# Sample attention's cached values: from held values and 16 moving columns to held weights and moving values

## The chip, the cores and the metric

The kernel runs on one core of a Trainium2 chip. The metric is the device time of one execution in microseconds (us), from the start of the program to its end. Times "before" are the median of three executions without a profiler, 2341.11 us (2338.23 to 2343.40 us). Beside them stands one execution taken by the hardware profiler; its span runs from the first to the last instruction. The engines are PE (TensorE: matmuls; PEld is its load of the held operand), DVE (VectorE), ACT (ScalarE), POOL (GpSimd) and SP (SyncE, which issues the DMAs of this kernel).

## The reference

One layer of an encoder works on two kinds of rows: a prompt of 2048 frames, and a sample of 8 running streams with 16 new frames each, 128 rows together. Each sample stream attends to 512 cached keys and values of its own and to its 16 new frames. There are two branches: differential attention (4 heads, two score maps each, values 128 wide) and stick-breaking attention (8 heads, values 64 wide). The branches are gated, merged, projected, added to the input and normed.

```python
w = p[:, :, 0] - lam * p[:, :, 1]
o = jnp.einsum('bhqk,bkhe->bqhe', w, v, preferred_element_type=jnp.float32)
...
a = jnp.where(mask, jnp.exp(log_a), 0.0)
o = jnp.einsum('bhqk,bkhd->bqhd', a, v, preferred_element_type=jnp.float32)
...
oa = diff_attention(qa, jnp.concatenate([cache_a_k[l], ka], axis=1),
                    jnp.concatenate([cache_a_v[l], va], axis=1), pos_s, kpos_s, lam)
ob = stick_breaking_attention(qb, jnp.concatenate([cache_b_k[l], kb], axis=1),
                              jnp.concatenate([cache_b_v[l], vb], axis=1), pos_s, kpos_s)
```

The change touches the product of weights and cached values (the two einsums) for the sample's streams. All other parts stay.

## The kernel before, in words

The kernel splits each fp32 operand into two fp16 parts, a high and a low one, and replaces one fp32 matmul by three fp16 ones (high x high, high x low, low x high). Work goes by 17 tiles of 128 rows: 16 of the prompt (`t < NT`) and one of the sample (`t == NT`). The attention of the prompt is done by eight units `u`: even units (`kind` 0) are one head of differential attention, odd ones (`kind` 1) two heads of stick-breaking attention. A first stage prepares the inputs, a second one projects and runs the prompt's attention, and the last one, from about 1780 us of the profile on, merges the branches and projects tile by tile. Its matmuls are L1315 (`branches`), the transposes L1165 (`transposed`) and L1344 (`output`); `wo`, `wb`, `wa` hold split weights or activations.

The sample's attention is threaded through that last stage. `sample` returns 13 lists of pieces for each unit. They are put on a `lane`, a unit starting 6 steps (`S_PERIOD`) after the one before it, and `aside` hands the 55 lane steps out over the first 13 tiles of the stage; `interleave` mixes them with the pieces of the tile. The framework's scheduler then fixes the order of instructions of each engine; each engine works through its queue in order. SP's queue holds all loads and stores of this stage, the transposing DMAs among them.

A unit's lane steps are these. Step 0, `fetch`: the unit's own sample rows are loaded (`dsam`) and the scale factors `dsf` computed (L736 to L738). Steps 0 to 3 load the cached keys, two streams at a time (`cache`, L747, tile `dc`, 512 KB), steps 5 to 8 the cached values in the same way; keys and values share three buffers `dc`. `keys` splits keys (`k16c`, L290 on ACT and L295 on DVE) and turns them with a transposing DMA (`dks`, L754). `scores_all` (step 6) computes scores. There (L772) the held operand is the query, padded to 32 columns in `qpad`, each for one of four groups of 32 columns of PE that belongs to 32 partitions of the result, and 512 columns of keys are moved. Softmax or stick-breaking follow; `turn` splits the weights and turns them with a transposing DMA (`dwt`, L580): keys on partitions, 128 sample rows on columns, 5 blocks of high parts and 5 of low parts (four cached blocks of 128 keys and the new rows). `values` (steps 6 to 9) splits the values (`v16c`).

`output_cached(i)` (steps 8 to 11) computes the product for two streams at a time. A cached block of values is held (128 keys by 128 columns for an even unit, by 64 for each head of an odd one) and the 16 columns of weights of one stream are moved; 12 matmuls (3 pairs of parts, 4 blocks) add up one stream of one head (L803). The result stands turned, value columns on partitions and sample rows on columns, in the only buffer of PSUM tag "t"; ACT scales its 32 columns into `ot` (L806). `finish` (step 12) computes the part of the new rows into `o` (`pv_block`, `natural`), turns `ot` back on PE (L815) and adds it on DVE (L816); `store` sends `o` to `o_d`, from where the sample's tile, the last but one of the stage, takes it.

Of the kernel before, what the change touches and what calls it, by code (L numbers as in the profile page):

```python
# [16 lines left out]
F32 = mybir.dt.float32  # L17
# [3 lines left out]
AF = mybir.ActivationFunctionType  # L21
ALU = mybir.AluOpType
# [3 lines left out]
P = 128  # L26
# [4 lines left out]
NS = 16  # L31
# [6 lines left out]
STICK = 14  # L38
# [25 lines left out]
C_MAS = C_MB + 128  # L64
C_MBS = C_MAS + 128
C_SEL = C_MBS + 128
C_N = C_SEL + 256


def shape_constants():  # L70
    half = 32
    inv = (10000.0 ** (-np.arange(half, dtype=np.float64) / half)).astype(np.float32)
    pos = np.concatenate([np.arange(SEQ), np.tile(PAST + np.arange(NS), NB)]).astype(np.float32)
    ang = (pos[:, None] * inv[None, :]).astype(np.float64)
    cos = np.cos(ang).astype(np.float32).reshape(17, P, half).transpose(1, 0, 2)
# [12 lines left out]
    return c  # L88
# [21 lines left out]
def layer_kernel(ctx: ExitStack, tc: tile.TileContext, a: dict):  # L110
# [6 lines left out]
    def act(**kw):  # L117
# [16 lines left out]
        "av": a["cache_a_v"][0].rearrange("b (j p) h e -> p (b j) (h e)", p=P),  # L134
        "bk": a["cache_b_k"][0].rearrange("b (j p) h d -> p (b j) (h d)", p=P),
        "bv": a["cache_b_v"][0].rearrange("b (j p) h d -> p (b j) (h d)", p=P),
    }
    outs = {
        "ak": (a["out_2"][0, 0].rearrange("s h c d -> s (h c d)"),
# [47 lines left out]
    def bank(tag, dt=F32):  # L187
        return ps.tile([P, 512 if dt == F32 else 1024], dt, tag=tag, name=f"ps_{tag}", bufs=BANKS[tag])
# [530 lines left out]
    def cache_column(name, h):  # L719
        return ("ak", "av", "bk", "bv").index(name) * 4 + h  # L720

    def sample(U, dec, qpad, cs):


        kind, h, t, sc, sq = U["kind"], U["h"], NT, U["sc"], U["sq"]
# [5 lines left out]
        def fetch():  # L731

            box["s"] = sam = dec.tile([P, 8, P], F16, tag="dsam", name="dsam", bufs=2)
            load(out=sam, in_=s_d[U["u"]])
            box["f"] = f = dec.tile([P, 3], F32, tag="dsf", name="dsf", bufs=2)
            V.tensor_scalar(out=f[:, 0:1], in0=ik, scalar1=sq[:, 1:2], scalar2=0.125, op0=ALU.mult, op1=ALU.mult)  # L736
            V.tensor_scalar(out=f[:, 1:2], in0=ik, scalar1=sq[:, 1:2], scalar2=-0.125, op0=ALU.mult, op1=ALU.mult)
            V.tensor_scalar(out=f[:, 2:3], in0=iv, scalar1=ls[:, 1:2] if kind == 0 else 2.0 ** -STICK, scalar2=None, op0=ALU.mult)  # L738

        def queries():  # L740
            for r in range(2):
# [2 lines left out]

        def cache(name, i):
            box[name, i] = kc = dec.tile([P, 8, P], F32, tag="dc", name="dc", bufs=3)
            load(out=kc, in_=caches[name][:, i * 8 : i * 8 + 8, h * P : (h + 1) * P])  # L747

        def keys(i):
            kc = box.pop((nk, i))  # L750
# [36 lines left out]
            box["v", i] = v16 = dec.tile([P, 8, 2, P], F16, tag="v16c", name="v16c", bufs=2)  # L787
            split(v16[:, :, 0, :], v16[:, :, 1, :], vc, sv, S)

        def output_cached(i):  # L790

            if i == 0:
                box["ot"] = dec.tile([P, P], F32, tag="ot", name="ot")
            vs = box.pop(("v", i))
            po = bank("t")
            for b in range(2):
                cols = slice((2 * i + b) * NS, (2 * i + b + 1) * NS)
                for c, job in enumerate(box["jobs"]):
                    r = slice(c * 64, c * 64 + 64) if kind == 1 else slice(0, P)
                    n = 0  # L800
                    for vf, wf in ((0, 0), (0, 1), (1, 0)):
                        for j in range(4):
                            T.matmul(po[r, cols], vs[:, b * 4 + j, vf, r], job["segs"][0]["wt"][:, wf * 5 + j, cols], start=(n == 0), stop=(n == 11))  # L803
                            n += 1
            c = slice(i * 32, i * 32 + 32)
            S.activation(out=box["ot"][:, c], in_=po[:, c], func=AF.Identity, scale=box["f"][:, 2:3])  # L806

        def finish():
            po = bank("s")
            vn = box["s"][:, 6:8, :].rearrange("p c (f d) -> p c f d", f=2)  # L810
            for job in box["jobs"]:
                pv_block(job, job["segs"][0], po, 4, vn, True, True)
            o = natural(U, t, po, dec)
            pt = bank("t")
            T.transpose(pt[:, 0:P], box["ot"], ident)  # L815
            V.tensor_tensor(out=o, in0=o, in1=pt[:, 0:P], op=ALU.add)  # L816
            store(U, t, o)

        def one(fn, *args):
# [460 lines left out]
    with ExitStack() as c2:  # L1280
# [81 lines left out]

        qpad = res.tile([P, 4, NB, 32], F16, name="qpad")
        G.memset(qpad, 0.0)

        lane = []
        for u in range(8):
            for i, pieces in enumerate(sample(units[u], dec, qpad, cs)):
# [58 lines left out]
```

## Time and profile before

| what | us |
|---|---|
| three executions without the profiler: median (lowest, highest) | 2341.11 (2338.23, 2343.40) |
| span of the profiled execution | 2337.1 |
| PE busy in it | 2121.6 (91%) |
| DVE busy | 1707.5 (73%) |
| ACT busy | 1663.1 (71%) |
| POOL busy | 661.3 (28%) |
| first and last start of L803 | 1874.4 and 2216.0 |

A profiled execution's time outside the span isn't recorded; the median lies 4.0 us above this span. A row of a group names its line, engine, operation, output and inputs, shapes (partitions x elements) and count. A matmul's own length in the profile includes its way through the array, so that neighbours overlap; what a matmul costs in a stream is the distance from one start to the next.

### The profile page before, as it was taken

Reading aid. Unit: us, or ns where it says so; the run is one execution under the profiler, and the core shown is the slowest. Engines: PE = TensorE matmul, PEld = TensorE weight load, DVE = VectorE, ACT = ScalarE, POOL = GpSimd, SP = SyncE. Lnnn points to the kernel's source line nnn. Section 1 sums busy time; section 2 is a strip of 40 time slices with the busy share of each in tenths; the row PEclk is TensorE's granted clock in tenths of the full one; section 3 lists DMA queues with packets and bytes.
Section 4 is the critical chain, followed back from the end, with each engine's and each line's share of the span. In section 5 each row is a group of like instructions: output and inputs, shape, how many; then the busy total and the mean of one; then the engine's idle time right before and its main releaser. Section 6 shows DMA issues by size and latency. Waiting matters only on the chain. (4 is left out here: it accounts for less than half of the span.)

```text
span 2337.1 us, 42708 instructions
## 1 busy us (share of the span) xinstructions
PE 2121.6 (91%) x15272; PEld 1144.0 (49%) x15272; DVE 1707.5 (73%) x3653; ACT 1663.1 (71%) x3292; POOL 661.3 (28%) x578
## 2 busy tenths in 40 slices
PE   5998898998989899899999979999995878989998
PEld 3654454545545445445545545554553444544443
DVE  4658765779875677978667797777788777777663
ACT  4968777787877778778677777866777656756541
POOL 1222022356300334731024474103345111121111
PEclk7999999999999999999999999999997988999999
DMA  9777659897895898867577777756677999999521
GB/s 333 275 214 180 152 118 272 179 193 168 212 210 126 216 204 192 179 178 192 134 191 176 185 168 186 195 146 150 146 171 166 285 254 233 257 245 236 155 98 53
DMA packets 834358, 445.35 MB, mean 191 GB/s; under 512 B 537210, under 2 KB 777130, under 8 KB 833632
## 3 DMA queue, kind: packets, MB, share of 16 engines
q1 hardware_dynamic: 833196, 442.24, 76.0%
q8 instruction: 119, 1.95, 0.4%
q14 instruction: 95, 0.78, 0.1%
q10 hardware_dynamic: 948, 0.39, 0.1%
HBM read 245.60 MB, written 69.24 MB: 135 GB/s over the span
## 5 line engine op out<-in xcount | busy, mean ns | idle before, releaser
L622 POOL TENSOR_TENSOR sc_p<-sc_p,sc_n 128x127 f32<-128x127 f32 (+7 forms) x192 | 313.8, 1638 | 826.5 <-DVE sc_n L616 812.2
L428 PE MATMUL ps_mm<-wb,hs 128*128 128x512 f16 x1632 | 414.5, 382 | 1.5 <-DMA hs<-hT_d 1.3
L428 PEld LDWEIGHTS <-hs 128*128 128x128 f16 x3120 | 274.4, 98 | 257.3 <-DMA hs<-hT_d 11.8
L428 PE MATMUL ps_mm<-wa,hs 128*128 128x512 f16 x1488 | 374.6, 382 | 9.8 <-DVE qbuf L463 6.4
L616 DVE TENSOR_TENSOR_SCAN sc_n<-ps_s,sc_n,zero_t 128x512 f32<-128x512 f32 x192 | 245.4, 1278 | 68.4 <-ACT ps_s L119 65.0
L639 PE MATMUL ps_s<-k,qst 128*128 128x512 f16 (+3 forms) x640 | 224.2, 351 | 37.9 <-DVE sc_n L616 29.9
L573 DVE TENSOR_TENSOR sc_n<-sc_p,sc_n 128x128 f16<-128x128 f32 (+7 forms) x192 | 212.7, 1112 | 58.1 <-ACT sc_n L572 57.6
L504 PEld LDWEIGHTS <-hs 128*128 128x128 f16 x1632 | 156.6, 98 | 188.3 <-ACT qst L532 6.2
L119 ACT ACTIVATE sc_p<-ps_s,usc 128x512 f32<-128x512 f32 (+3 forms) x320 | 204.8, 640 | 30.2 <-PE ps_s L640 25.3
L640 PE MATMUL ps_s<-k,qst 128*128 128x512 f16 (+3 forms) x640 | 224.2, 352 | 0.0
L572 ACT CAST sc_n<-sc_p 128x128 f16<-128x128 f32 (+7 forms) x192 | 155.5, 813 | 78.5 <-POOL sc_p L622 76.9
L700 PE MATMUL ps_o<-v,wt 128*128 128x128 f16 x1088 | 171.5, 225 | 32.6 <-DMA wt<-sc_n 32.2
L119 ACT ACTIVATE ps_s<-ps_s,usc 128x512 f32<-128x512 f32 (+3 forms) x328 | 200.0, 610 | 0.0
L504 PE MATMUL ps_t<-wa,hs 128*128 128x512 f16 x816 | 192.9, 383 | 7.6 <-ACT qst L532 6.0
L504 PE MATMUL ps_t<-wb,hs 128*128 128x512 f16 x816 | 191.9, 380 | 1.2 <-DVE qst L532 0.8
L1344 PE MATMUL ps_o<-wo,wb 128*128 128x512 f16 x816 | 186.5, 383 | 4.1 <-ACT wb L1166 4.1
L701 PE MATMUL ps_o<-v,wt 128*128 128x64 f16 x1088 | 157.9, 197 | 0.0
L700 PEld LDWEIGHTS <-wt 128*128 128x128 f16 x1088 | 105.1, 101 | 98.1 <-DMA wt<-sc_n 45.1
L558 DVE TENSOR_SCALAR_CACHE_REDUCE sc_p<-ps_s,usc 128x512 f32<-128x512 f32 (+3 forms) x160 | 106.3, 665 | 42.4 <-PE ps_s L640 31.7
L616 DVE TENSOR_TENSOR_SCAN sc_n<-ps_s,zero_t 128x128 f32<-128x128 f32 (+3 forms) x128 | 104.1, 814 | 44.0 <-ACT ps_s L119 43.4
L558 DVE TENSOR_SCALAR_CACHE_REDUCE sc_n<-ps_s,usc 128x512 f32<-128x512 f32 (+3 forms) x160 | 106.3, 665 | 36.9 <-PE ps_s L640 26.3
L701 PEld LDWEIGHTS <-wt 128*128 128x128 f16 x1088 | 103.1, 100 | 54.3 <-issue 1.1
(360 smaller groups left out, 4493.6 us busy)
## 6 DMA issues: line engine op xcount, KB each, us to landing
hs<-hT_d SPq DMA_DIRECT2D x130, 512.0 KB, 4.2
g_d<-gt SPq DMA_DIRECT2D x68, 256.0 KB, 4.2
wb<-g_d SPq DMA_DIRECT2D x26, 512.0 KB, 4.8
out_dram<-pr SPq DMA_DIRECT2D x204, 64.0 KB, 2.3
o_d<-o SPq DMA_DIRECT2D x136, 64.0 KB, 2.2
hs<-o_d SPq DMA_DIRECT2D x17, 512.0 KB, 5.6
out_dram<-x SPq DMA_DIRECT2D x17, 512.0 KB, 2.8
wide<-in_w_ada_dram SPq DMA_DIRECT2D x8, 1024.0 KB
```

What stands on the lines that cost most here:

```text
L119: i = S.activation(**kw)
L428: T.matmul(box["p"], box["h"][:, hi, k, :], U["w"][k][:, wi, :], start=(n == 0), stop=(n == 3 * KT - 1))
L504: T.matmul(box["g"][:, 0:gw], box["h"][:, hi, k, :], U["wg"][k // per][:, k % per, wi, :], start=(j == 0), stop=(j == 3 * KT - 1))
L558: V.tensor_scalar(out=dst[:, lo : lo + n], in0=p[:, 0:n], scalar1=sc_pos, scalar2=None, op0=ALU.mult, op1=ALU.max, accum_out=job["mx"][:, ...
L573: V.tensor_tensor(out=lo, in0=src, in1=hi, op=ALU.subtract)
L616: V.tensor_tensor_scan(out=dst[:, lo : lo + n][:, ::-1], data0=src[:, 0:n][:, ::-1], data1=zero_t[:, 0:1].to_broadcast([P, n]), initial=fi ...
L622: G.tensor_tensor(out=p[:, 0:m], in0=p[:, 0:m], in1=n[:, 1 : m + 1], op=ALU.mult)
L639: T.matmul(p[:, 0:n], qst[:, c, :], kk[:, c, 0:n], start=True, stop=False)
L640: T.matmul(p[:, 0:n], qst[:, 2 + c, :], kk[:, c, 0:n], start=False, stop=not diag)
L700: T.matmul(po[:, c * P : (c + 1) * P], wt[:, wj, :], vt[:, c, :, :], start=first, stop=False)
L701: T.matmul(po[:, c * P : c * P + 64], wt[:, nb + wj, :], vt[:, c, 0, :], start=False, stop=last)
L1344: T.matmul(po, st["y"][:, yi * 8 + k, :], wo[j * 4 + k // 2][:, wi, k % 2, :], start=(n == 0), stop=(n == 3 * KT - 1))
```

## The change

Cached values are loaded by block of 128 keys, for all 8 streams, instead of by pair of streams with all four blocks; the new views are `values_by_block`. `output_cached(j)` then treats block `j`. Held are 32 columns of the weights, the 32 sample rows of a pair of streams `i`, on the group of 32 PE columns that belongs to these rows; moved are the values of both streams of the pair, 2 x 128 columns for an even unit and 2 x 64 for each head of an odd one. All four calls of a unit add into one bank of tag "t", from the first call to `finish`. In that bank each sample row has the product with its own stream's values and with those of its neighbour. `parity`, two new columns of constants loaded once, is 1 where a row's stream is even, or odd. `dsf` has four columns, the last two being the scale factor times `parity`; with these `finish` adds the right half for each row in two DVE instructions. The evictions into `ot`, the tile `ot`, the transpose and the addition after it are gone.

```diff
-C_N = C_SEL + 256
+C_PAR = C_SEL + 256
+C_N = C_PAR + 2
...
+    for r in range(2):
+        c[:, C_PAR + r] = np.arange(P) // NS % 2 == r
...
+    values_by_block = {
+        "av": a["cache_a_v"][0].rearrange("b (j p) h e -> p j b (h e)", p=P),
+        "bv": a["cache_b_v"][0].rearrange("b (j p) h d -> p j b (h d)", p=P),
     }
...
-    def sample(U, dec, qpad, cs):
+    def sample(U, dec, qpad, cs, parity):
...
-            box["f"] = f = dec.tile([P, 3], F32, tag="dsf", name="dsf", bufs=2)
+            box["f"] = f = dec.tile([P, 4], F32, tag="dsf", name="dsf", bufs=2)
...
-            V.tensor_scalar(out=f[:, 2:3], in0=iv, scalar1=ls[:, 1:2] if kind == 0 else 2.0 ** -STICK, scalar2=None, op0=ALU.mult)
+            V.tensor_scalar(out=f[:, 2:4], in0=parity, scalar1=iv, scalar2=ls[:, 1:2] if kind == 0 else 2.0 ** -STICK, op0=ALU.mult, op1=ALU.mult)
...
-            load(out=kc, in_=caches[name][:, i * 8 : i * 8 + 8, h * P : (h + 1) * P])
+            if name == nv:
+                load(out=kc, in_=values_by_block[name][:, i, :, h * P : (h + 1) * P])
+            else:
+                load(out=kc, in_=caches[name][:, i * 8 : i * 8 + 8, h * P : (h + 1) * P])
...
-        def output_cached(i):
-
-            if i == 0:
-                box["ot"] = dec.tile([P, P], F32, tag="ot", name="ot")
-            vs = box.pop(("v", i))
-            po = bank("t")
-            for b in range(2):
-                cols = slice((2 * i + b) * NS, (2 * i + b + 1) * NS)
+        def output_cached(j):
+
+            if j == 0:
+                box["po"] = bank("t")
+            vs = box.pop(("v", j))
+            w = P // heads
+            for vf, wf in ((0, 0), (1, 0), (0, 1)):
                 for c, job in enumerate(box["jobs"]):
-                    r = slice(c * 64, c * 64 + 64) if kind == 1 else slice(0, P)
-                    n = 0
-                    for vf, wf in ((0, 0), (0, 1), (1, 0)):
-                        for j in range(4):
-                            T.matmul(po[r, cols], vs[:, b * 4 + j, vf, r], job["segs"][0]["wt"][:, wf * 5 + j, cols], start=(n == 0), stop=(n == 11))
-                            n += 1
-            c = slice(i * 32, i * 32 + 32)
-            S.activation(out=box["ot"][:, c], in_=po[:, c], func=AF.Identity, scale=box["f"][:, 2:3])
+                    for i in range(4):
+                        rows = slice(i * 32, i * 32 + 32)
+                        T.matmul(box["po"][rows, c * P : c * P + 2 * w], job["segs"][0]["wt"][:, wf * 5 + j, rows],
+                                 vs[:, 2 * i : 2 * i + 2, vf, c * w : c * w + w],
+                                 start=(j == 0 and vf == 0 and wf == 0 and c == 0), stop=(j == 3 and wf == 1 and c == heads - 1))
...
-            pt = bank("t")
-            T.transpose(pt[:, 0:P], box["ot"], ident)
-            V.tensor_tensor(out=o, in0=o, in1=pt[:, 0:P], op=ALU.add)
+            ov = o.rearrange("p (c d) -> p c d", c=heads)
+            pc = box["po"][:, 0:256].rearrange("p (c r d) -> p r c d", c=heads, r=2)
+            for r in range(2):
+                V.scalar_tensor_tensor(out=ov, in0=pc[:, r, :, :], scalar=box["f"][:, 2 + r : 3 + r], in1=ov, op0=ALU.mult, op1=ALU.add)
             store(U, t, o)
...
+        parity = res.tile([P, 2], F32, name="parity")
+        load(out=parity, in_=a["shapes"][:, C_PAR : C_PAR + 2])
```

More of the change, by code (lines that the diff above doesn't have):

```diff
@@ L136, in layer_kernel @@
         "bv": a["cache_b_v"][0].rearrange("b (j p) h d -> p (b j) (h d)", p=P),
+    }
+    values_by_block = {
+        "av": a["cache_a_v"][0].rearrange("b (j p) h e -> p j b (h e)", p=P),
+        "bv": a["cache_b_v"][0].rearrange("b (j p) h d -> p j b (h d)", p=P),
     }
@@ L1364, in layer_kernel @@
         G.memset(qpad, 0.0)
+        parity = res.tile([P, 2], F32, name="parity")
+        load(out=parity, in_=a["shapes"][:, C_PAR : C_PAR + 2])
         lane = []
         for u in range(8):
-            for i, pieces in enumerate(sample(units[u], dec, qpad, cs)):
+            for i, pieces in enumerate(sample(units[u], dec, qpad, cs, parity)):
                 if S_PERIOD * u + i == len(lane):
```

## The prediction

> **What bounds the kernel now.** Three unprofiled runs took 2338.23 to 2343.40 us (median 2341.11). The profiled execution spans 2337.1 us, 4.0 us under that median; durations below come from this one execution, the change is summed against its 2337.1 us, and the 4.0 us are added again at the end. What a measurement of this kernel can tell from no change I take as 0.2%, 4.7 us.
>
> The edited steps all lie in the last stage, so I read first the busy times by stretch (bounds; length; busy time and count of PE, PEld, DVE, ACT, POOL; granted clock; DMA share; GB/s).
>
> ```profile
> PE 2121.6 (91%) x15272; PEld 1144.0 (49%) x15272; DVE 1707.5 (73%) x3653; ACT 1663.1 (71%) x3292; POOL 661.3 (28%) x578
> ...
> 1780.00:1900.00 120.00, 95.54 (x664) 49.06 (x663) 93.28 (x163) 72.30 (x93) 28.86 (x19) 0.87 1.00 255
> 1900.00:2000.00 100.00, 84.54 (x733) 44.65 (x734) 77.69 (x153) 69.83 (x103) 16.36 (x12) 0.86 0.95 237
> 2000.00:2100.00 100.00, 90.04 (x810) 47.42 (x808) 74.45 (x168) 61.22 (x88) 18.39 (x12) 0.93 1.00 249
> 2100.00:2222.00 122.00, 112.34 (x1015) 59.70 (x1014) 83.59 (x195) 73.87 (x107) 18.76 (x13) 0.94 0.71 195
> 2222.00:2326.00 104.00, 102.04 (x559) 49.24 (x557) 50.70 (x119) 36.78 (x50) 16.23 (x12) 1.00 0.22 75
> ```
>
> After 2222 us, when the sample work is over, PE is busy for 102.04 of 104 us: whatever is earlier there ends the kernel earlier. From 2100 to 2222 PE has 112.34 of 122 and the DMA share has fallen to 0.71: nearly PE-bound. From 1780 to 2100 PE has 270 of 320 us at a granted clock near 0.9, while the DMA engines stand at 0.95 to 1.00: there two resources set the pace, and time saved on PE can turn into waiting for DMA.
>
> Next, what PE waited for from 1780 to 2222 us, and what ACT waited for (us in total, times, longest):
>
> ```profile
> PE ps_o L700 <- DMA wt<-sc_n: 12.4, 5, 4.8
> PE ps_t L803 <- DMA dwt<-dsc: 9.5, 5, 4.0
> PE ps_s L772 <- DMA dks<-k16c: 8.5, 4, 3.6
> PE ps_t L803 <- ACT ot L806: 8.0, 6, 2.3
> ```
>
> ```profile
> ACT k16c L290 <- DMA dc<-in_cache_b_k_dram: 28.8, 11, 6.1
> ...
> ACT k16c L290 <- DMA dc<-in_cache_a_k_dram: 27.7, 9, 8.1
> ...
> ACT v16c L290 <- DMA dc<-in_cache_b_v_dram: 7.4, 3, 4.1
> ```
>
> The fourth row is the one that the change touches: L803 of one call waits for the eviction at L806 of the call before, because bank "t" exists once. ACT, which must evict, is itself held up by cache loads; keys (28.8 and 27.7 us) far more than values (7.4 us).
>
> **The matmuls.** L803 holds cached values and moves 16 columns: 24 matmuls a call for an even unit, 48 for an odd one, 16 calls of each kind. From PE's timeline (start, length, group), one call of each with what follows it, a full score step L772, and L815:
>
> ```profile
> 1874.44 0.75 PE L803 MATMUL ps_t<-dwt,v16c 128*128 128x16 f16 x24
> 1875.04 0.77 PE L1165 MATMUL ps_s<-id,hs 128*128 128x128 f16 x11
> ```
>
> ```profile
> 2118.86 1.39 PE L803 MATMUL ps_t<-dwt,v16c 128*64 128x16 f16 x48
> 2120.18 3.84 PE L1344 MATMUL ps_o<-wo,wb 128*128 128x512 f16 x17
> ```
>
> ```profile
> 2170.97 0.27 PE L815 MATMUL ps_t<-ident,ot 128*128 128x128 f32 x1
> 2171.08 0.38 PE L1315 MATMUL ps_mm<-wa,wb 128*128 128x512 f16 x1
> ...
> 2174.31 0.59 PE L1315 MATMUL ps_mm<-wb,wb 128*128 128x512 f16 x2
> 2174.84 1.91 PE L772 MATMUL ps_s<-dks,qpad 128*32 128x512 f16 x32
> 2176.68 10.53 PE L1344 MATMUL ps_o<-wo,wb 128*128 128x512 f16 x48
> 2187.05 1.06 PE L1165 MATMUL ps_s<-id,wa 128*128 128x128 f16 x16
> ```
>
> Start to start, 24 matmuls take 0.60 us (25 ns each), 48 take 1.32 us (27.5 ns each), a transpose 0.11 us. L1344 moves 512 columns in 10.37/48 = 0.216 us. L772 is the very shape of the new code: 32 held columns on four column groups. Its 32 matmuls take 1.84 us where one after another they would take 6.9; that is 8 groups of four at 0.216 plus 0.11 us on leaving. Two L1315 just before it take 0.53 instead of 0.43 us, so entering costs 0.10 us.
>
> The new call of an even unit is 12 matmuls of 256 columns: 3 groups at 0.108 us, 0.32, plus 0.2 for entering and leaving, 0.52 us. Against 0.60 that saves 0.08 (an even call so far pays neither side). Bounds: 0.42 if entering is free, 0.62 if a group takes 0.14, so +0.18 to -0.02 us a call. 16 calls: 1.3 us (2.9 to -0.3).
>
> The new call of an odd unit is 24 matmuls of 128 columns. If only the moved columns count, 6 groups at 0.054 plus 0.10 on leaving make 0.42 us (the 64-column calls already pay something at both sides, so no entry is added). If loading weights sets the pace as it does now, 24 pairs at 27.5 ns plus 0.10 make 0.76 us. No row shows 32 held columns with so few moved. Halving the held columns of the 27.5 ns row should shorten the load and four groups overlap, so I take the middle, 0.55 us. Saved: 0.77 us a call, 12.3 us in all (14.4 to 9.0).
>
> The Trainium skill ("TensorE: Matmul & The Clock Gate", section on LDWEIGHTS) gives a rule that speaks against the change: loading weights takes the number of held columns over 1.2 in ns, so 27 ns for 32 columns and 107 ns for four groups, twice the 54 ns of the moved columns; by it an odd call would be 0.74 us and the saving 9.3 us. The same rule would ask 53 ns for each 64-column load of the x48 row, which shows 27.5 ns a pair, so this trace does not bear its figure out, and the sum above goes without it.
>
> The transposes L815 go: 8 times 0.11, 0.9 us. PE's work falls by 14.5 us (bounds 9.6 to 18.2).
>
> **ACT, DVE, the wait.** From 1780 to 2230 us by line (count, then busy us and mean ns, then idle before):
>
> ```profile
> L806 ACT ACTIVATE ot<-ps_t,dsf 128x32 f32<-128x32 f32 x32 | 9.0, 282 | 9.4 <-PE ps_t L803 9.4
> ```
>
> ```profile
> L816 DVE TENSOR_TENSOR o<-o,ps_t 128x128 f32<-128x128 f32 x8 | 2.3, 282 | 1.5 <-PE ps_t L815 1.4
> ...
> L681 DVE SCALAR_TENSOR_TENSOR o<-ps_s,usc,ob 128x128 f32<-128x128 f32 x4 | 1.4, 341 | 0.0
> ```
>
> All 32 evictions go: 9.0 us less on ACT, hidden behind PE but for the 8.0 us in which PE waited for them; the four calls now add into one bank and none waits for ACT. Instead `finish` reads the bank twice on DVE with the instruction of L681: 2 x 341 for 282 ns, 0.40 us a unit, 3.2 us in all. DVE is busy about three quarters of the time, and DVE's work seldom releases PE here, so I charge a fifth, 0.6 us. The bank is now held from a unit's first call to that read; the next unit's first call comes two lane steps, half a tile, later, so I expect no wait there. L738 stays one short instruction.
>
> SP's and DVE's queues where the load of `parity` comes in, and the smallest loads and stores of the page (count, KB, us to landing):
>
> ```profile
> 1807.12 0.34 SPq L1382 DMA_DIRECT2D gt<-in_final_g_dram  x1
> ...
> 1807.98 0.44 SPq L747 DMA_DIRECT2D dc<-in_cache_a_k_dram  x1
> ```
>
> ```profile
> 1810.93 0.20 DVE L738 TENSOR_SCALAR dsf<-s_c,ls_i 128x1 f32<-128x1 f32 x1
> ...
> 1811.35 0.73 DVE L1317 SCALAR_TENSOR_TENSOR wb<-ps_mm,fuy,wb 128x512 f32<-128x512 f32 x1
> ```
>
> ```profile
> out_dram<-pr SPq DMA_DIRECT2D x204, 64.0 KB, 2.3
> o_d<-o SPq DMA_DIRECT2D x136, 64.0 KB, 2.2
> ```
>
> The load, two numbers a partition, costs SP one issue (0.34 us) ahead of the first cache load; the first L738 waits for it, and behind that in DVE's queue stands the eviction L1317, for which PE waits. It costs 0 if it is issued some 3 us before 1810.93, and up to a landing, 2.3 us, if not; I take 0, as it stands before the cache load of 1807.98.
>
> **What of it reaches the end.** The calls by shape from 2100 to 2222 us:
>
> ```profile
> L803 PE MATMUL ps_t<-dwt,v16c 128*64 128x16 f16 x336 | 11.0, 183 | 5.2 <-DMA dwt<-dsc 3.1 <-ACT ot L806 1.9
> ...
> L803 PE MATMUL ps_t<-dwt,v16c 128*128 128x16 f16 x96 | 3.1, 169 | 3.5 <-ACT ot L806 1.9 <-DMA dwt<-dsc 1.0 <-DVE v16c L295 0.5
> ...
> L815 PE MATMUL ps_t<-ident,ot 128*128 128x128 f32 x3 | 0.9, 287 | 0.0
> ```
>
> That is 7 odd calls, 4 even ones and 3 transposes: 7 x 0.77 + 4 x 0.08 + 3 x 0.11 = 6.0 us, counted in full. Of the 3.8 us that PE waited there for L806 I count half, 1.9, since ACT was late for its loads and the next PE work also needs ACT. Before 2100 lie 9 odd calls, 12 even ones, 5 transposes and 4.2 us of that wait: 8.4 + 4.2 = 12.6 us. With the DMA share at 1.00 between none and all could count; PE is busy 270 of 320 us but the keys' loads hold ACT; I take a third, 4.2 us. Sum: 6.0 + 1.9 + 4.2 - 0.6 = 11.5 us. 2337.1 - 11.5 + 4.0 gives 2329.6 us. With the lower bounds, nothing before 2100 and no wait it is 7 x 0.56 + 0.3, 4 us; with the upper bounds after 2100 (7.3 us), all 3.8 us of the wait there and half of what lies before (6.3 us) it is 17 us. The likeliest case's own range is 2324 to 2337 us.
>
> **The rivals.**
> First, the gain is swallowed: PE only arrives earlier at waits for the turned weights and keys (9.5 and 8.5 us above), which are paced by DMA and by ACT's and DVE's splits. For it: the DMA share, and the granted clock of 0.86, which falls where PE idles. Against it: the stretch after 2100. Then 6.0 us come free there, half of it goes into the 4.1 us of waits for `dwt`, and 3 us remain: 2338 us. Chance 0.15.
>
> Second, all is realised: 14.5 + 8.0 = 22.5 us, 2319 us. Against it: DMA at 1.00 for 320 us. Chance 0.11.
>
> Third, and slower: the value loads. They move the same 512 KB, but one block of keys from eight sequences instead of four blocks from two. Sizes and landing times now, from 1700 to 2250 us:
>
> ```profile
> dc<-in_cache_a_k_dram SPq DMA_DIRECT2D x16, 512.0 KB, 4.4
> dc<-in_cache_a_v_dram SPq DMA_DIRECT2D x16, 512.0 KB, 5.7
> dc<-in_cache_b_k_dram SPq DMA_DIRECT2D x16, 512.0 KB, 3.9
> dc<-in_cache_b_v_dram SPq DMA_DIRECT2D x16, 512.0 KB, 5.1
> ```
>
> Values and keys share three buffers `dc`, so a late value load delays the next keys, which ACT waits for. If the wider stride makes each of the 32 value loads 1.2 us longer and half of it reaches the pace, that is 19 us, less 11.5: 2349 us. It decides from 0.7 us a load on. Against it: pieces of 512 bytes and their number stay the same, and ACT waits little for values now. Chance 0.07.
>
> Fourth, the change doesn't do what it says: the column groups do not overlap with so little to move. Then an even call is 12 x 0.108 + 0.2 = 1.5 us and an odd one 24 x 0.054 + 0.1 = 1.4: 14.4 + 1.3 us more on PE, of which by the shares above 8 arrive, less 3 of the wait removed: 2346 us. L772 speaks against it. Chance 0.04.
>
> Fifth, smaller memory for `ot` and the new `parity` move the later buffers by half a kilobyte, and the instruction order shifts; at the start of the stage (1780 to 1900, 24 us of idle PE) that can go either way by some 8 us from no gain. Chance 0.08, mostly slower.
>
> **The numbers.** The likeliest has the remaining 0.55. Faster by over 0.2%: nine tenths of it, the second, a fifth of the fifth, 0.62. Within: a tenth of the likeliest, most of the first, a little of the fourth and fifth, 0.21. Slower: 0.17. The range for 8 in 10 runs from the second rival to the fourth, 2319 to 2346 us.
>
> **What would show it.** The cached output as x12 and x24 groups with 128*32, an odd call near 0.55 us and an even one near 0.52 start to start; no wait of PE for ACT in them; no L806 and L815; two DVE instructions of 0.34 us per unit; waits for `dwt` and `dks` grown by a few us; the stretch after the sample work unchanged at 104 us but begun 8 to 15 us earlier. I am wrong if an odd call takes over 0.9 us, if value loads land later than 7 us, or if the waits for DMA grow by as much as PE lost.

## The result, and the profile after

| kernel | median of runs, us | lowest to highest | runs | span of its profile |
|---|---|---|---|---|
| before, on the same chip | 2341.38 | 2335.99 to 2348.26 | 12 | 2337.1 |
| after | 2341.60 | 2338.62 to 2346.54 | 12 | 2343.9 |

The ratio is 1.0004, 95% interval 0.9994 to 1.0013: no change. Forecast were 2329.6 us, 11.5 us of gain. The profiled execution of after took 2345.66 us, near the top of its range, that of before 2341.11 us, at its median; so some 4 us of what sets the two profiles apart is this one execution's. In the code of after, lines behind the edit stand lower: the cached output is L810, the scores L782, the splits L297 (ACT) and L302 (DVE), the branches' matmuls L1322, the output's L1351, the transposes L1172.

First the matmuls themselves, in PE's timeline of after (start, length, group): two calls of an even unit, one right behind the other, then one call of an odd unit, each with what follows.

```profile
1969.23 0.84 PE L810 MATMUL ps_t<-v16c,dwt 128*32 128x256 f16 x24
1970.00 0.23 PE L703 MATMUL ps_s<-dsam,dwt 128*128 128x128 f16 x1
...
2018.58 0.52 PE L810 MATMUL ps_t<-v16c,dwt 128*32 128x128 f16 x24
2019.03 0.39 PE L1322 MATMUL ps_mm<-wa,wa 128*128 128x512 f16 x1
```

Start to start, an odd call takes 0.45 us (1.32 before) and a pair of even calls 0.77, 0.39 each (0.60 before). The column groups overlap: six groups of four in 0.45 us are 75 ns a group, where four 128-column matmuls one after another would take four times 54 (a quarter of the 216 ns of 512 columns). Over 16 calls of each kind that is 13.9 + 3.4 us, with 0.9 for the transposes 18.2 us less, at most: a call that other matmuls interrupt pays more. PE's busy time in the page's first part fell by 17.5 us, and the two large terms of the saving came out larger than forecast.

```profile
PE 2104.1 (90%) x14688; PEld 1119.9 (48%) x14688; DVE 1714.2 (73%) x3661; ACT 1656.7 (71%) x3260; POOL 664.1 (28%) x578
```

So PE was relieved as meant, and the end did not move. The busy times by stretch of after show what took the place (columns as in the prediction), with the whole of the sample's work in one row at the end:

```profile
1780.00:1900.00 120.00, 94.83 (x634) 47.49 (x634) 92.49 (x166) 73.47 (x94) 31.12 (x19) 0.90 0.97 251
1900.00:2000.00 100.00, 75.99 (x571) 36.63 (x572) 79.29 (x160) 63.87 (x87) 18.22 (x12) 0.88 1.00 242
2000.00:2100.00 100.00, 82.61 (x609) 39.25 (x609) 73.74 (x162) 64.76 (x86) 15.88 (x11) 0.94 0.96 241
2100.00:2222.00 122.00, 105.41 (x828) 51.50 (x827) 89.55 (x200) 71.41 (x94) 20.39 (x15) 0.97 0.72 202
...
1780.00:2222.00 442.00, 358.84 (x2639) 174.87 (x2640) 335.07 (x685) 273.51 (x359) 85.60 (x56) 0.92 0.90 233
```

The four rows of before have 382.46 us of PE work in the same 442 us: 59.5 us idle. After, it is 358.84: 83.2 us idle. PE lost 23.6 us of work there and gained as much idle time; 17.5 us of it are gone for good, the rest now lies outside these bounds. The DMA share stands at 0.96 to 1.00 up to 2100 us, as it did.

What PE waited for from 1780 to 2230 us, after:

```profile
PE ps_o L707 <- DMA wt<-sc_n: 14.9, 7, 4.8
PE ps_t L810 <- DMA dwt<-dsc: 9.4, 8, 3.2
PE ps_s L782 <- DMA dks<-k16c: 9.3, 5, 3.7
PE ps_s L1172 <- ACT wa L1173: 7.7, 1, 7.7
...
PE ps_t L810 <- ACT v16c L297: 5.6, 2, 4.2
PE ps_t L810 <- DVE v16c L302: 4.8, 5, 1.4
```

The 8.0 us of waits for the eviction are gone. The cached output now waits 10.4 us for its split values (0.5 us before), and the three DMA waits (33.6 us in all, 30.4 before) are slightly longer. Behind the split values stand the loads, in what ACT waited for, after:

```profile
ACT k16c L297 <- DMA dc<-in_cache_b_k_dram: 29.1, 13, 4.8
ACT k16c L297 <- DMA dc<-in_cache_a_k_dram: 24.2, 12, 7.3
...
ACT v16c L297 <- DMA dc<-in_cache_b_v_dram: 9.1, 5, 4.2
ACT v16c L297 <- DMA dc<-in_cache_a_v_dram: 7.5, 5, 2.5
```

Keys are waited for as before (56.5 us then, 53.3 now), values 16.6 us; before, the one row quoted had 7.4 and the row of the other cache this:

```profile
ACT v16c L290 <- DMA dc<-in_cache_a_v_dram: 1.5, 2, 1.2
```

That is a hint at the value loads, no more: a wait shows what came last, not what it costs the end. The experiments had to price it.

### The profile page after: what moved, and what is told of

Read it like the earlier page. It is cut to its first block, busy times and chain, and to the rows that moved or that the text cites. A ratio compares the mean times of both kernels' runs of the same rounds, so it can differ in the third digit from the quotient of the medians.

```text
span 2343.9 us, 41533 instructions
## 1 busy us (share of the span) xinstructions
PE 2104.1 (90%) x14688; PEld 1119.9 (48%) x14688; DVE 1714.2 (73%) x3661; ACT 1656.7 (71%) x3260; POOL 664.1 (28%) x578
## 5 line engine op out<-in xcount | busy, mean ns | idle before, releaser
L1351 PE MATMUL ps_o<-wo,wb 128*128 128x512 f16 x816 | 186.1, 382 | 5.6 <-ACT wb L1173 5.6
```

Source lines behind the costliest of these rows:

```text
L1351: T.matmul(po, st["y"][:, yi * 8 + k, :], wo[j * 4 + k // 2][:, wi, k % 2, :], start=(n == 0), stop=(n == 3 * KT - 1))
```

## The experiments

All runs have five rounds against the kernel before on the same chip. "us" in the table is (ratio - 1) x 2341, the change against the kernel before; each kernel was executed 5 to 12 times, and an interval reaches 2 to 4 us to either side. Differences of two kernels are taken between these figures. "By block" are value loads as in the changed kernel, "by pair" those of the kernel before.

| label | kernel | ratio, 95% interval | us |
|---|---|---|---|
| (after) | the change | 1.0004, 0.9994 to 1.0013 | +0.9 |
| b_vblock | before, values by block | 1.0013, 0.9999 to 1.0026 | +3.0 |
| b_third | before, a third of the cached output's matmuls | 0.9918, 0.9904 to 0.9931 | -19.2 |
| a_half | after, half of each cache load | 0.9914, 0.9899 to 0.9929 | -20.1 |
| a_nolow | after, no low parts of values | 0.9971, 0.9958 to 0.9984 | -6.8 |
| b_onebank | before, one eviction a unit | 1.0014, 1.0003 to 1.0025 | +3.3 |
| a_third | after, a third of the matmuls | 0.9979, 0.9964 to 0.9995 | -4.9 |
| b_half | before, half of each cache load | 0.9962, 0.9946 to 0.9979 | -8.9 |
| a_spaced | after, calls at before's places | 0.9986, 0.9972 to 1.0000 | -3.3 |
| a_spacedT | after, calls at b_third's places | 0.9990, 0.9976 to 1.0003 | -2.3 |
| a_s14 | after, lane over 14 tiles | 0.9985, 0.9971 to 1.0000 | -3.5 |
| a_bystream | after, values by pair | 0.9943, 0.9929 to 0.9957 | -13.3 |
| b_third_vblock | b_third, values by block | 0.9987, 0.9972 to 1.0002 | -3.0 |
| a_dma8 | after, a value load as 8 of one stream | 1.0016, 1.0004 to 1.0028 | +3.7 |
| a_4x2 | after, tiles of 4 streams by 2 blocks | 0.9956, 0.9940 to 0.9973 | -10.3 |
| a_odd | the change for odd units alone | 0.9974, 0.9960 to 0.9989 | -6.1 |
| a_dma4 | after, a value load as 4 of two streams | 0.9993, 0.9978 to 1.0008 | -1.6 |

The theories were: PE's time is not what counts, since DMA sets the pace (A); the splits on ACT and DVE set it (C); the new order of calls in PE's queue eats the saving (D); the value loads by block are dear (B, later G). A letter in a quoted expectation stands for its theory; E, F and H are explained where they stand.

**Does PE's time count, and do the loads?** One part of the change alone, and one suspected resource relieved at a time.

b_vblock, the new loads in the kernel before:

```diff
-            load(out=kc, in_=caches[name][:, i * 8 : i * 8 + 8, h * P : (h + 1) * P])
+            if name == nv:
+                load(out=kc, in_=values_by_block[name][:, i, :, h * P : (h + 1) * P])
+            else:
+                load(out=kc, in_=caches[name][:, i * 8 : i * 8 + 8, h * P : (h + 1) * P])
```

> The kernel before, with its cached values loaded by block of keys for eight streams, as the changed kernel loads them; the old matmuls then multiply the wrong blocks, the amount of work is unchanged. Theory A (the stage with the sample's lane is paced by DMA and by the splits fed from it, so that time saved on PE turns into waiting): the same time as before within 5 us. Theory B (the new loads cost what PE saves): 10 us or more slower.

+3.0 us (-0.2 to +6.1). Taken alone, in the kernel where PE sets the pace, the loads seem nearly innocent.

b_third, in before only the product of high parts:

```diff
-                    for vf, wf in ((0, 0), (0, 1), (1, 0)):
+                    for vf, wf in ((0, 0),):
...
```

> The kernel before, with only the product of high parts left in the cached output: 384 matmuls of L803 in place of 1152, some 24 us less on PE, evictions, loads and splits as they were. Theory A: within 5 us of before, PE's idle time in the lane grows by what was taken out. If PE's work paced the lane: 15 us or more faster.

-19.2 us, with 768 matmuls of 25 to 27.5 ns (some 20 us) taken from PE and all loads as they were. PE's time does count, nearly in full; A in its pure form falls.

a_half, half of the bytes of each key and value load, split twice:

```diff
-                load(out=kc, in_=values_by_block[name][:, i, :, h * P : (h + 1) * P])
+                load(out=kc[:, 0:4, :], in_=values_by_block[name][:, i, 0:4, h * P : (h + 1) * P])
...
-            split(v16[:, :, 0, :], v16[:, :, 1, :], vc, sv, S)
+            vv = v16.rearrange("p (a x) f n -> p a x f n", a=2)
+            split(vv[:, :, :, 0, :], vv[:, :, :, 1, :], vc[:, 0:4, :].unsqueeze(1).to_broadcast([P, 2, 4, P]), sv, S)
```

> The changed kernel, with half of each cached block loaded (256 of 512 KB, 64 loads) and each loaded half split twice, so that ACT, DVE, PE and the transposing DMAs do the same work with other numbers. Theory A: the DMA share from 1780 to 2100 falls from about 1.0 to about 0.85 and the time by 15 to 35 us. Theory C (the splits on ACT and DVE pace the lane): within 6 us of the changed kernel.

b_half, the same in the kernel before:

> The kernel before, with half of each cached block loaded and each loaded half split twice, as in a_half (2323.7 us); the result has other numbers. If the loads are what swallows the change, PE's time counts here and this lies 6 us or more above a_half. If the change itself costs what it saves, this lies within 4 us of a_half.

-20.1 and -8.9 us. Loads count in both kernels, more in the changed one; with half the bytes the change is worth 20.1 - 8.9 = 11.2 us, close to what was forecast for it. So the saving is there, and the loads hide it.

a_nolow, no low parts of values, in after (a third of the cached output's matmuls goes with them):

```diff
-            split(v16[:, :, 0, :], v16[:, :, 1, :], vc, sv, S)
+            S.activation(out=v16[:, :, 0, :], in_=vc, func=AF.Identity, scale=sv)
...
-            for vf, wf in ((0, 0), (1, 0), (0, 1)):
+            for vf, wf in ((0, 0), (0, 1)):
```

> The changed kernel without the low parts of cached values: 32 instructions of DVE (some 41 us) and a third of the cached output's matmuls are left out, loads as they were. Theory A: at most 6 us faster. Theory C: 15 us or more faster.

-6.8 us, 7.7 below after, for 41 us less on DVE and some 4.5 us less on PE (a third of 13.4). That lies between the two ranges of the expectation; the splits on DVE can be worth little. ACT's split stayed, so for ACT this run says nothing; a_half and b_half, whose splits all stayed, got faster all the same.

a_third, the changed kernel with the product of high parts alone:

```diff
-            for vf, wf in ((0, 0), (1, 0), (0, 1)):
+            for vf, wf in ((0, 0),):
...
```

> The changed kernel, with only the product of high parts in the cached output (192 of 576 matmuls), beside the same cut in the kernel before (b_third, 2324.6 us): in both the cached output costs PE little, so what differs is all else in the change. Theory E: 2316 to 2325 us, at or below b_third. Theory D: 2331 us or more.

5.8 us below after, for some 9 us less on PE (two thirds of 16 x 0.45 + 16 x 0.39). It lies in the range of theory D and 14.3 us above b_third, where the same was left out of the kernel before: what swallows the gain is not the time of the product's matmuls. The order, D, was the first suspect.

**The order.** In the trace of before the four calls of unit 0 come behind 219, 232, 247 and 264 matmuls of the stage's own; in after behind 219, 219, 238 and 240 (the x24 group of two even calls above is such a pair). Three runs on that, and one on the evictions.

b_onebank, before with one bank held by a unit, evicted once:

```diff
+                box["po"] = bank("t")
-            po = bank("t")
+            po = box["po"]
...
-            c = slice(i * 32, i * 32 + 32)
-            S.activation(out=box["ot"][:, c], in_=po[:, c], func=AF.Identity, scale=box["f"][:, 2:3])
+            if i == 3:
+                S.activation(out=box["ot"], in_=po[:, 0:P], func=AF.Identity, scale=box["f"][:, 2:3])
```

> The kernel before, with one part of the change alone: the four calls of a unit write into one bank of tag t that is evicted once, at the end (8 evictions of 128 columns in place of 32 of 32); matmuls, loads and transposes stay. The scheduler then puts the second and fourth call of a unit right behind the first and third in PE's queue. Theory D (without the evictions between them the calls stand too early in PE's queue, and PE waits in them for values): 3 to 12 us slower than before, PE's waits in L803 for the splits of values grow from 0.5 us to 5 us or more. Theory E (only PE's time counts): the same or up to 6 us faster, as PE's waits for L806 and 7 us of ACT are gone.

+3.3 us, and PE's waits for the split values on DVE grew from 0.5 to 6.2 us, as theory D had it, at the low end of its range: the waits for evictions that this removes were worth nothing by themselves, or the order that came with it took back as much and more.

a_spaced and a_spacedT, after with scheduling edges (order only, no waits) that put the first matmul of each call behind so many of the stage's own:

```diff
+    targets = [[219, 232, 247, 264], [323, 336, 352, 352], [432, 451, 462, 485], [552, 571, 590, 600], [690, 711, 720, 742], [816, 837, 842, 871], [984, 1005, 1010, 1032], [1105, 1128, 1152, 1176]]
...
+                            if 0 < targets[U["u"]][j] <= len(mains):
+                                tc.add_manual_dep(m.ins, mains[targets[U["u"]][j] - 1].ins.name, NOSYNC, reason="order")
```

> The changed kernel with scheduling edges and nothing else: the first matmul of each call is kept behind the main matmul (L1322, L1351) behind which the same call stood in the kernel before, so that a unit's four calls stand apart in PE's queue again. Theory D (bunched calls): 2328 to 2336 us, PE's waits for the splits of values fall from 10 us to under 3. Theory F (the order of these calls does not matter; DMA swallows what PE saves): within 4 us of the changed kernel.

> The same with the places that the calls have in b_third (2324.6 us), ten to thirty main matmuls later. Theory D: 2322 to 2334 us, at or below a_spaced. Theory F: within 4 us of the changed kernel.

a_s14, the lane handed out over 14 tiles, the sample's tile last:

```diff
-S_TILES = 13
+S_TILES = 14
...
-    tiles = list(range(NT - 1)) + [NT, NT - 1]
+    tiles = list(range(NT + 1))
```

> The changed kernel with the lane handed out over 14 tiles in place of 13, the sample's tile last in place of last but one: the loads of the lane spread over one more tile of main matmuls, after which DMA is idle now. If loads swallow PE's gain: 2328 to 2336 us, the tail some 3 us longer counted in. If the calls' order does: within 4 us of the changed kernel.

-3.3, -2.3 and -3.5 us, all with intervals that reach to 1.0000 or beyond. In a_spaced PE's waits for split values fell from 10.4 to 0.8 us, as meant, and the time hardly followed. Against after the three are worth 3 to 4 us, some 7 at the ends of their intervals, not the 11.5 missing: D falls as the main cause. a_s14 is also a miss for the loads: had one more tile given them room, 2328 to 2336 us were expected; its median, 2339.50, lies in the range given for the other case. Its DMA share from 1800 to 2180 us is 0.98, as full as in after (0.97), so the room was not there; why is not known.

**The loads, where PE is relieved.** a_bystream is after with the value loads by pair, all else as it is.

```diff
-            if name == nv:
+            if False:
```

> The changed kernel with one part undone: cached values are loaded by pair of streams with four blocks each, as before, all else as changed; the new matmuls then meet the wrong values, the amount of work is unchanged. Theory G (DMA is full from 1800 to 2170, and loads by block make its 512-byte pieces some nanoseconds longer, which takes back what PE saves): 2326 to 2336 us, 6 us or more below the changed kernel. Theory H (the loads' order is worth the 3 us of b_vblock at most): within 4 us of the changed kernel.

b_third_vblock, the edits of b_third and b_vblock together:

> b_third (2324.6 us: the kernel before, only the product of high parts) with the loads of values by block of keys; wrong blocks are multiplied, the amount of work is that of b_third. Theory G: 2331 us or more. Theory H: 2322 to 2328 us.

a_bystream takes 13.3 us less than before, 14.2 less than after, and in its trace every call of the cached output stands behind the same number of the stage's own matmuls as in after: with the order on PE unchanged, the loads alone are worth the 14.2 us. Its last cached output starts at 2208.3 us, that of after at 2217.7. b_third_vblock takes 16.2 us more than b_third, again in the same order. The same edit that cost 3.0 us in the kernel before costs 14 to 16 us where PE has less to do. The DMA view from 1800 to 2180 us (packets, MB, mean rate; packets by size) of after, a_bystream, b_third and b_third_vblock, in this order:

```profile
DMA packets 167446, 94.36 MB, mean 248 GB/s; under 512 B 86246, under 2 KB 152806, under 8 KB 167416
```

```profile
DMA packets 168480, 96.12 MB, mean 253 GB/s; under 512 B 86562, under 2 KB 153250, under 8 KB 168450
```

```profile
DMA packets 172029, 96.99 MB, mean 255 GB/s; under 512 B 89919, under 2 KB 156607, under 8 KB 171999
```

```profile
DMA packets 166633, 93.96 MB, mean 247 GB/s; under 512 B 86290, under 2 KB 151994, under 8 KB 166604
```

With loads by pair the engines move 253 to 255 GB/s, by block 247 to 248, at shares of 0.97 to 0.98 in each of the four. By stretch, a_bystream (columns as above, to be set against the first three rows of after):

```profile
1780.00:1900.00 120.00, 94.08 (x619) 47.24 (x621) 96.70 (x167) 74.47 (x96) 31.91 (x21) 0.89 0.97 254
1900.00:2000.00 100.00, 78.16 (x605) 37.34 (x596) 81.58 (x168) 69.87 (x95) 19.89 (x13) 0.87 0.97 249
2000.00:2100.00 100.00, 86.02 (x686) 41.51 (x685) 79.06 (x166) 67.44 (x89) 17.17 (x12) 0.99 1.04 258
```

Over 380 us 2 to 3% are 8 to 12 us, the size of what is lost. The rate alone does not tell cause from effect, since a kernel that ends earlier also moves more in fixed bounds: a_nolow and a_third, by block but with less other work, have 250 and 251 GB/s. The pairs of runs do, as they differ in the loads alone. The kernel before, by pair, moves no more than by block:

```profile
DMA packets 165937, 94.53 MB, mean 249 GB/s; under 512 B 84477, under 2 KB 151037, under 8 KB 165903
```

What ACT waited for values: in b_third and, below it, in b_third_vblock:

```profile
ACT v16c L290 <- DMA dc<-in_cache_b_v_dram: 12.5, 5, 5.3
ACT v16c L290 <- DMA dc<-in_cache_a_v_dram: 5.1, 4, 2.6
```

```profile
ACT v16c L294 <- DMA dc<-in_cache_b_v_dram: 20.6, 6, 7.3
ACT v16c L294 <- DMA dc<-in_cache_a_v_dram: 11.9, 6, 4.2
```

17.6 us became 32.5; after has 16.6 where a_bystream has 10.4 (6.6 and 3.8).

**Which property of the loads.** A cached row of one key is 2 KB (4 heads of 512 bytes), so pieces that follow each other within a partition's load lie 256 KB apart by pair (next block) and 1 MB apart by block (next stream).

a_dma8, each value load of after as eight, one for each stream:

```diff
-                load(out=kc, in_=values_by_block[name][:, i, :, h * P : (h + 1) * P])
+                for b in range(8):
+                    load(out=kc[:, b, :], in_=values_by_block[name][:, i, b, h * P : (h + 1) * P])
```

> The changed kernel with each of its 32 value loads given as eight loads of one stream each (64 KB, pieces of 512 bytes that lie 2 KB apart, where the whole load steps 1 MB from piece to piece). Theory 'stride' (the value loads by block are dear because pieces that follow each other lie 1 MB apart; loading by pair of streams, 256 KB apart, was worth about 14 us): the cost goes, about 2332 us or a few us below, ratio to before 0.990 to 0.995. Theory 'order of need' (a block needs pieces of all eight streams, whichever way they are fetched): no change from the changed kernel, 2340 to 2346 us, ratio 0.998 to 1.001. Should 224 more loads cost SP's queue time that the loads behind them lack, it is slower than before, above 2350 us.

+3.7 us, in none of the three ranges given: the gain that theory 'stride' asked for did not come. By itself that is no answer, since the engines were no longer kept full. Its busy times by stretch from 1900 to 2100 us:

```profile
1900.00:2000.00 100.00, 74.40 (x547) 34.32 (x543) 74.35 (x150) 58.90 (x78) 15.27 (x11) 0.90 0.88 227
2000.00:2100.00 100.00, 85.41 (x629) 40.90 (x621) 75.13 (x156) 62.45 (x84) 14.60 (x10) 0.95 0.91 242
```

The DMA share is 0.88 and 0.91 where it was 1.00 and 0.96: 224 more loads of 64 KB seem to bring a limit of their own; which one is not shown.

a_4x2, value tiles of four streams and two blocks, each loaded by four loads of one stream; a call covers two column groups and two blocks:

```diff
...
-                load(out=kc, in_=values_by_block[name][:, i, :, h * P : (h + 1) * P])
+                for b in range(4):
+                    load(out=kc[:, 2 * b : 2 * b + 2, :], in_=values_by_block[name][:, i % 2 * 4 + b, i // 2 * 2 : i // 2 * 2 + 2, h * P : (h + 1) * P])
...
-                    for i in range(4):
-                        rows = slice(i * 32, i * 32 + 32)
-                        T.matmul(box["po"][rows, c * P : c * P + 2 * w], job["segs"][0]["wt"][:, wf * 5 + j, rows],
-                                 vs[:, 2 * i : 2 * i + 2, vf, c * w : c * w + w],
+                    for k in range(2):
+                        for i in range(2):
+                            rows = slice(j % 2 * 64 + i * 32, j % 2 * 64 + i * 32 + 32)
+                            T.matmul(box["po"][rows, c * P : c * P + 2 * w], job["segs"][0]["wt"][:, wf * 5 + j // 2 * 2 + k, rows],
+                                     vs[:, 4 * i + k : 4 * i + k + 3 : 2, vf, c * w : c * w + w],
...
```

> The changed kernel with value tiles of four streams and two blocks in place of eight streams and one block, each given as four loads of one stream (128 KB, two pieces 256 KB apart); a call of output_cached then works on two column groups and two blocks, all sums as before. Theory 'stride': the dear step of 1 MB is gone, while two column groups in place of four give back a part of PE's saving (an odd call between 0.45 us and 0.9 us, so up to 7 us over 16 calls): 2332 to 2339 us, ratio 0.993 to 0.998. Theory 'order of need' or cost by the number of loads: 2341 to 2348 us, ratio 0.999 to 1.002.

a_dma4, the control: as many loads of the same size in after, pieces 1 MB apart:

```diff
-                load(out=kc, in_=values_by_block[name][:, i, :, h * P : (h + 1) * P])
+                for b in range(0, 8, 2):
+                    load(out=kc[:, b : b + 2, :], in_=values_by_block[name][:, i, b : b + 2, h * P : (h + 1) * P])
```

> The changed kernel with each of its 32 value loads given as four loads of two streams each (128 KB, two pieces 1 MB apart): number and size of the loads as in the kernel with tiles of four streams and two blocks, the steps between pieces and the matmuls as in the changed kernel. Theory 'stride' (1 MB between pieces is what is dear, and the tiles of four streams by two blocks gained by their 256 KB): 2339 to 2347 us, ratio 0.998 to 1.001, some 8 us above the kernel with those tiles. Theory 'size of the loads' (four loads of 128 KB share the engines better with the transposes and the other loads than one of 512 KB, whatever the steps): 2331 to 2336 us, ratio 0.994 to 0.997, as with those tiles.

-10.3 us for a_4x2 and -1.6 for a_dma4, intervals apart. The number and size of loads is the same, and a_4x2 even pays more on PE, as its timeline shows for an odd call (0.78 us start to start against 0.45):

```profile
2101.72 0.85 PE L812 MATMUL ps_t<-v16c,dwt 128*32 128x128 f16 x24
2102.50 0.61 PE L1324 MATMUL ps_mm<-wb,wb 128*128 128x512 f16 x2
```

The rates from 1800 to 2180 us, a_4x2 and then a_dma4:

```profile
DMA packets 167781, 95.75 MB, mean 252 GB/s; under 512 B 85939, under 2 KB 152499, under 8 KB 167749
```

```profile
DMA packets 170171, 94.61 MB, mean 249 GB/s; under 512 B 90056, under 2 KB 155401, under 8 KB 170139
```

So it is the places in memory that count, not the size of the loads. Which property of them is not settled: in a_4x2 the step inside a load is shorter, and a whole tile also spreads over four streams in place of eight. a_dma8, with no step of 1 MB inside a load but tiles spread over eight streams, did not gain, though with its engines less full. a_4x2 holds the whole computation and is faster than both kernels.

a_odd, even units as before, odd ones as after (even units keep L803, L806 and L815):

```diff
...
-            if name == nv:
+            if name == nv and kind == 1:
...
+        output_cached = output_blocks if kind == 1 else output_streams
...
```

> The changed product and the value loads by block for the four odd units alone; even units load and compute as before, with evictions, transpose and addition. Odd calls carry most of PE's saving (0.87 of about 1.1 us for a call of each kind). Theory 'stride': half of its cost of about 14 us goes and 10 to 12 us of PE's saving stay: 2334 to 2340 us, ratio 0.995 to 0.999, below the changed kernel. A theory in which the shared bank of the even units or the changed order matters, not the loads, has no reason for a gain: 2341 to 2345 us.

-6.1 us, within the range given: half of the loads by pair, and the calls kept that carry most of PE's saving.

## Why the prediction was wrong

**The step that failed** is the price of the value loads. The prediction set it to nothing in the sum, and left it to the third rival with a chance of 0.07, on two arguments: "pieces of 512 bytes and their number stay the same, and ACT waits little for values now". The first is true and does not settle it: with the same pieces in another order the rate fell from 253 to 248 GB/s. The second looked at the wrong moment: ACT's waits for values, 8.9 us in before, are 17.6 in b_third, where only PE's work was taken away. PE's work had covered the loads, and the change itself takes that cover away. Shown by runs: 14.2 us (a_bystream against after), 16.2 us (b_third_vblock against b_third), 3.0 us where PE covers it (b_vblock). The third rival named the right loads and put 19 us on them; that each lands later, as it had it, the landing times below do not show. Per load, 14.2/32 is 0.44 us at the end.

**What was right.** The gain without that step: 11.5 us forecast, 13.3 measured (a_bystream), 11.2 with half the bytes. That the sum comes so close is in part luck, as PE's terms were too small and the share of them that arrives was guessed. Its terms: an odd call 0.55 forecast (called the middle of 0.42 and 0.76, which is 0.59; with 0.59 the sum would be 0.4 us less), 0.45 measured; an even one 0.52 and 0.39; transposes 0.9 as priced; in all 14.5 forecast and up to 18.2 measured, the upper bound. The Trainium skill's rule for loading weights ("TensorE: Matmul & The Clock Gate", section on LDWEIGHTS), by which an odd call would take an estimated 0.74 us, does not fit the measured 0.45. The instructions in `finish` came out as priced, 345 ns each for the 341 taken (two a unit):

```profile
L823 DVE SCALAR_TENSOR_TENSOR o<-ps_t,dsf,o 128x128 f32<-128x128 f32 x16 | 5.5, 345 | 0.2
```

**The share realised.** "A third" of what lies before 2100 was a guess between none and all. b_third realised 19.2 of some 20 us. There the loads go by pair, and the rate rose with PE's relief, from 249 to 255 GB/s.

**The waits.** The eviction's 8.0 us went, 3.3 of them counted within the 11.5 (1.9, and a third of 4.2). b_onebank, which spares three of four evictions, was 3.3 us slower, so how much of that term arrived is not shown by itself.

**The other rivals.** That DMA swallows the gain (2338 us, 0.15) has the right resource and the wrong reason: DMA was full before as well, but it had rate in reserve by pair. That column groups don't overlap is refuted by the 75 ns a group. Of the fifth (0.08), the order is put at 3 to 4 us by a_spaced and a_s14; the moved buffers stand in a_bystream as well, which has its gain.

**The signs to look for.** None of the three signs of being wrong appeared: an odd call takes 0.45 us, PE's three waits for DMA grew by 3.2 us, and the values' median landing time, where the view has one, is 6.1 us, not over 7. The last, the sign for the third rival, was too coarse. From 1700 to 2250 us after has:

```profile
dc<-in_cache_a_v_dram SPq DMA_DIRECT2D x16, 512.0 KB, 6.1
```

5.7 before, 0.4 us more: that is the size of the whole loss when it is multiplied by 32, and far from the 1.2 us asked for. a_bystream shows 6.1 too, so a median landing time among full queues cannot tell these loads apart at all. The rate differs, but it needs a pair of runs to be read.

**What stays open.** Which property of the places in memory costs time, and where within the memory or the DMA engines. Worked out from the packets in the traces, a 512-byte packet from 1800 to 2160 us took on average:

```
kernel            values    mean ns of a 512-byte packet
b_third           by pair   29.68
b_third_vblock    by block  31.56
a_bystream        by pair   29.85
after             by block  30.14
```

There are some 62,000 of them on 16 engines, so a nanosecond is 3.9 us: 7 us of the 16 in the first pair, 1 of the 14 in the second. The direction holds in all runs with whole value loads: 29.5 to 29.9 ns in the four kernels by pair, 30.1 to 31.6 in the eight by block. a_4x2 and a_dma4, 8.7 us apart, have 29.87 and 29.96, so most of their difference shows elsewhere. The packets of 256 bytes, which are not the value loads' own, took longer too: 24.7 ns in b_third_vblock against 23.9, and 25.1 in after against 23.8; with some 80,000 of them on 16 engines that is 4 and 6 us. But before, by pair, has 25.0 as well, so this is not put down to the loads. Smaller steps, or another split of a_4x2's loads, were not tried.

## What to carry to other kernels

A cost that measures as nothing under the present bottleneck must be priced again in the kernel that the change makes: test it with the bottleneck relieved (here by leaving matmuls out), not in the kernel as it stands. Where DMA engines are full, the places in memory that a load walks through are part of its price, even when bytes, pieces and median landing times stay the same. A layout that suits the matmuls half way and keeps the loads cheap (here four streams by two blocks) can be worth more than the one that suits the matmuls best.

## What the runs showed of the hardware that was not expected

- 32 loads of 512 KB in 512-byte pieces cost 14 to 16 us more at the end by block (1 MB between a partition's pieces) than by pair (256 KB) where PE was relieved, and 3.0 us in the kernel before. The engines moved 247 to 248 GB/s against 253 to 255 in these pairs, at shares of 0.97 to 0.98.
- Splitting a load of 512 KB into eight of 64 KB came with a fall of the engines' share from 1.00 to 0.88 in the stretch from 1900 us; four of 128 KB did not hinder a_4x2's gain.
- Matmuls with 32 held columns and 128 moved overlap on four column groups down to 75 ns for a group of four, entering and leaving included; on two groups 24 of them take 0.78 us in place of 0.45.
